# All splits on VectorE, the residual's product in PSUM, and a square with a scalar operand

## The chip, the cores and the metric

One core of a Trainium2 chip runs the whole program. The metric is device time in microseconds of one execution; three runs of the kernel before took 1109.92, 1103.96 and 1104.01 us, median 1104.01.

## What is computed

256 tokens of width 1024 go through two layers of a first block and one layer of a second, all in fp32. A layer of the first block is a mixer (a gated delta rule over four heads beside a dilated attention over eight) and a feed-forward part with a depthwise convolution, each between two norms:

```python
for l in range(2):
    h = rmsnorm(x, pre_mix_norm[l])
    h = hybrid_mixer(h, ...)                   # products with w_in, chunks, attention, w_out
    x = x + rmsnorm(h, post_mix_norm[l])
    h = rmsnorm(x, pre_ffn_norm[l])
    h = conv_glu_ffn(h, ffn_up[l], ffn_conv[l], ffn_conv_bias[l], ffn_down[l])
    x = x + rmsnorm(h, post_ffn_norm[l])
hn = rms_norm(x, mix_norm_g)                   # the second block
x = x + concat(gla(hn), conv(hn), diff_attention(hn)) @ w_out_2
x = x + hier_moe(rms_norm(x, ffn_norm_g))      # best of 4 groups, then 2 of its 4 experts
```

## The kernel before

The stages follow one another: mixer1, ffn, mixer1, ffn, mixer2, moe. Every product is made with both operands cut into a rounded head and the rest, its tail: `mm3` issues three matmuls, head by head (L404), head by tail (L405) and tail by head (L406). A weight tile of 128 x 1024 comes by one DMA on the queue of SyncE into a raw tile `wr` (in the MoE also into `yh`, `yl`, `grow` or `hres`); ScalarE copies the head `wh` (L382), and then VectorE or GpSimd subtracts it from the raw tile and so makes the tail `wl` (L383). This subtraction is the split. Heads and tails have five buffers each.

Who makes a split is set by numbers at the top. `POOLED0 = 2` and `POOLED = 5` give GpSimd the first splits of `tok_first`, with which a mixer or feed-forward stage begins; `POOL1 = 10` and `POOL2 = 2` give it every tenth of the other splits of mixer1 and every second of mixer2; in the MoE it has all four of expert 0's first matrix, one of four (`KPOOL = (1,)`) of the 15 other experts', and the rows themselves (`XPOOL = 2`).

Between two stages stands a boundary, for each of the two token tiles (the first rows, the second rows): ScalarE sums the squares of the stage's output, which lies in two PSUM banks (L415), VectorE multiplies that output by a gain and writes the product to `hres` in SBUF (L487), takes a reciprocal root in a chain of one-column instructions (`rsqrt1`, L342 to L350, with the square y * y at L344), and adds the scaled product to the residual `x` (L491). TensorE transposes the new rows (L326), ScalarE and VectorE make their heads and tails (`xh` L358, `xl` L359), and `tok_first` multiplies: first five weight tiles with the first rows (30 matmuls), then the same with the second rows. The last products of the stage before, for the second rows, are held back to run while the first rows go through the boundary. There are four such boundaries; the MoE begins with a residual step of its own (`route`, L1568).

The program's text lists several chains and one stream of filling products in one order (`Weave`); the framework then lays out each engine's queue from that order and from estimated durations. An engine runs its queue strictly in order.

Of the kernel before, what the change touches and what calls it, by code (L numbers as in the profile page):

```python
# [10 lines left out]
F32 = mybir.dt.float32  # L11
# [26 lines left out]
AFTER = 4  # L38
KPOOL = (1,)
GAT = 1  # L40
XPOOL = 2
CUT0 = ((0, 512),)
CUT1 = ((512, 768), (768, 1024))
YUP = True
RSQ = (1.0, -0.5, 0.37499722695340487, -0.3125009091063101, 0.27502146815610246, -0.24676164253236588)
HOLD = None
LAG = True
# [6 lines left out]
LAGE = 2  # L54
POOLED0 = 2
FIRST = 1
# [7 lines left out]
OUT2 = (4, 5, 6, 7, 2, 3, 0, 1)  # L64
POOLED = 5
POOL1 = 10
POOL2 = 2
POOLF = 0
# [129 lines left out]
class Weave:  # L198
    """Lays several dependent chains and one stream of filling work into one trace order."""

# [47 lines left out]
def emit(ctx, tc, A, out, stop=None, dbg=None):  # L248
# [89 lines left out]
    def rsqrt1(ss, scale, o=None):  # L338
        """1 / sqrt(sum * scale + EPS) of one value a partition, whose sum comes in two parts."""
        c = tmp([P, 5], tag="rs1")  # L340
        u, y, q, e, v = (c[:, i:i + 1] for i in range(5))
        V.tensor_scalar(u, ss[:, 0:1], ss[:, 1:2], EPS / scale, op0=OP.add, op1=OP.add)  # L342
        V.tensor_scalar(y.bitcast(I32), u.bitcast(I32), -0.5, 1597463007.0, op0=OP.mult, op1=OP.add)
        V.tensor_tensor(q, y, y, op=OP.mult)  # L344
        V.tensor_scalar(e, q, u, 1.0, op0=OP.mult, op1=OP.subtract)
        V.tensor_scalar(v, e, RSQ[5], RSQ[4], op0=OP.mult, op1=OP.add)
        for i in (3, 2, 1, 0):
            V.tensor_scalar(v, v, e, RSQ[i], op0=OP.mult, op1=OP.add)
        r = v if o is None else o
        V.tensor_scalar(r, v, y, scale ** -0.5, op0=OP.mult, op1=OP.mult)  # L350
        return r

    def split(h, l, src, gain=None, eng=V):
        if gain is None:
            SC.copy(h, src)
            eng.tensor_tensor(l, src, h.bitcast(F32), op=OP.subtract)
        else:
            i = SC.activation(h, src, AF.Identity, scale=gain)  # L358
            j = V.scalar_tensor_tensor(l, src, gain, h.bitcast(F32), op0=OP.mult, op1=OP.subtract)  # L359
            return i.ins, j.ins  # L360
# [10 lines left out]
    def weight(ap, eng=None, first=False, raw=None, to=None):  # L371
        if eng is None:
            share[1] += 1
            eng = G if share[0] and share[1] % share[0] == 0 else V
        if raw is None:
            raw = raw_tile()
            nc.sync.dma_start(raw, ap)
        h, l = to or (wp.tile([P, 1024], F32R, name=nm("wh"), tag="wh", bufs=WH),
                      wp.tile([P, 1024], F32R, name=nm("wl"), tag="wl", bufs=WH))
        last = gate.pop() if gate else None  # L380
        with tc.issue_after(last) if last else ExitStack():
            heads[:] = [(V.tensor_copy if first else SC.copy)(h, raw).ins]  # L382
        eng.tensor_tensor(l, raw, h.bitcast(F32), op=OP.subtract)  # L383
        return h, l
# [8 lines left out]
    def narrow_gen(p, w, xT):  # L393
        """The products of a few columns; rows n and on of the output hold the low part's share."""
        xh, xl = xT
        n = w.shape[2]
        for k in range(KT):
            T.matmul(p[:n, :S], w[:, k, :], xh[:, k, :], start=k == 0, stop=False)
            T.matmul(p[:n // 2, :S], w[:, k, :n // 2], xl[:, k, :], start=False, stop=k == KT - 1)
            if k % 4 == 3:  # L400
                yield 0.9
# [16 lines left out]
    def rows_in(t, xT, a, g, gain, done):  # L418
        """The residual step of token tile t, and its new rows, transposed and split."""
        xh, xl = xT  # L420
# [22 lines left out]
    def row_scales(nv, done, lag):  # L443
        """What the next norm scales the rows by: per row, and the same spread over the partitions."""
        rv, hv, R = nv
# [34 lines left out]
    def residual(t, a, g):  # L480
        """x += rmsnorm(a) * g on token tile t."""
        ss = square_sum(lambda n: a[t][n], 2)
        h2 = tmp([P, 2, 512], tag="hres", bufs=1)
        hs = [h2[:, n] for n in range(2)]
        for n in range(2):
            with tc.issue_after(marks[0][HOLD[n]][1]) if t and HOLD and HOLD[n] is not None else ExitStack():
                V.tensor_tensor(hs[n], a[t][n], g[n], op=OP.mult)  # L487
        r = rsqrt1(ss, 1.0 / D)
        for n in range(2):
            ns = slice(n * 512, (n + 1) * 512)  # L490
            V.scalar_tensor_tensor(x[:, t, ns], hs[n], r, x[:, t, ns], op0=OP.mult, op1=OP.add)  # L491

# [20 lines left out]
    def tok_first(ps, chunks, xT, done, end, mid=None, ahead=None):  # L513
        """Two groups of products of token rows; those of the first rows go ahead of the second rows' norm."""
        xh, xl = xT
# [617 lines left out]
    def mixer2(before, held, a0):  # L1133
# [149 lines left out]
        def gla():  # L1283
# [23 lines left out]
            def level_x(X, half, t):  # L1307
                """The keys' and queries' factors of four levels on token tile t; the last level reaches over the tiles."""
                c0 = half * (4 + t)
# [189 lines left out]
    def onehot(o, v, idx):  # L1499
        """The first greatest of four, as a one-hot row; and its value."""  # L1500
        n = v.shape[1]
# [10 lines left out]
    def moe(held, a):  # L1512
# [26 lines left out]
        def gather(gp, ps, t):  # L1539
            """Token tile t's share of the rows of groups 2 gp and 2 gp + 1."""  # L1540
            for n, src in enumerate((xsh, xsl)):
# [20 lines left out]
        def route():  # L1562
            for t in range(NT):
# [41 lines left out]
                if t == 1:  # L1605
                    gather(0, got, 1)
                    yield (1.8, 0.1)

        early = [weight(A["egu"][0, kk], G if kk % 2 else V,
                        to=[tmp([P, D], F32R, tag=tag, bufs=2) for tag in ("yh", "yl")]) for kk in range(EARLY)]  # L1610
        whl = tmp([P, NT, 2, 5], F32R, tag="whl", bufs=1)

        def shares(t):
            """What each expert of its group gives to a row; the softmax's sum over four cancels in the two greatest's shares."""
            yield lambda: ("goh", t) in done
# [42 lines left out]
        def slot_values(p, g):  # L1658
            """What the tokens give to the slots of a group: an expert's share times the row's scale, and the scale."""
            for t in range(NT):  # L1660
                T.matmul(p, sel[:, t, g, :], whl[:, t].rearrange("p j e -> p (j e)"), start=t == 0, stop=t == NT - 1)
# [30 lines left out]
        def up(e, between):  # L1692
# [3 lines left out]
            for kk in range(4):  # L1696
                if e == 0 and kk < EARLY:
                    w = early[kk]
                else:
                    with later(2 if e == 1 and kk < AFTER else 0):  # L1700
                        w = weight(A["egu"][e, kk], G if e == 0 or kk in KPOOL else V, raw=raws.pop(("up", e, kk), None))
                wh, wl = (v.rearrange("p (k c) -> p k c", k=2) for v in w)
# [57 lines left out]
        def rest():  # L1760
            """The tokens of a group past its 128 slots; no more than one group has any."""
            g0 = nc.values_load(firsti[0:1, 1:2], min_val=0, max_val=12,
# [169 lines left out]
```

## Time and profile before

| | us |
|---|---|
| median of three runs | 1104.01 |
| span of the profiled execution | 1100.8 |
| TensorE busy | 1052.8 |
| VectorE busy | 904.2 |
| ScalarE busy | 634.5 |
| GpSimd busy | 209.9 |
| mean granted TensorE clock | 0.960 |

The profile is of one execution; its span runs from the first instruction to the last, so it is a little shorter than the time of a run. Busy time is a sum over stages with different limits; a stage is read from its own window.

### The profile page before, as it was taken

To read this page: it belongs to the slowest core of one execution; us is meant where nothing else is said; L and a number is where in the kernel's file an instruction comes from. 1 tells how busy PE (TensorE), PEld (TensorE's weight loads), DVE (VectorE), ACT (ScalarE), POOL (GpSimd) and SP (SyncE) were. 2 spreads that over 40 slices of the span, in tenths; PEclk is the share of its full clock that TensorE was granted. 3 is DMA by queue.
4 is the path that set the end of the run, shared out by engine and by line. 5 is a ranking of instruction groups with operands and counts; after the bars stand their busy time and mean duration, and the time that the engine had idled before them with its cause. 6 is when DMAs were issued, how large, how long until landed. Compare 5 with 4: busy or idle time off the path is not lost.

```text
span 1100.8 us, 17299 instructions
## 1 busy us (share of the span) xinstructions
PE 1052.8 (96%) x6156; PEld 900.5 (82%) x6156; DVE 904.2 (82%) x2073; ACT 634.5 (58%) x1139; POOL 209.9 (19%) x175
## 2 busy tenths in 40 slices
PE   8999999999999899999899999998899997999997
PEld 7879877899999788887679999996777776887785
DVE  6797797798888879868797988888889768888886
ACT  6554455666655665535466665556554234787773
POOL 3510004100000462000140000004423415123231
PEclk9999998999999999999989999999889679999999
DMA  8642025555555453401437556555532036398892
GB/s 318 216 134 77 2 94 177 190 190 174 189 179 188 153 191 117 133 21 39 153 118 225 174 180 187 189 188 157 163 106 77 20 114 233 102 333 320 320 348 89
DMA packets 51997, 181.07 MB, mean 164 GB/s; under 512 B 6050, under 2 KB 7491, under 8 KB 51907
## 3 DMA queue, kind: packets, MB, share of 16 engines
q1 hardware_dynamic: 51186, 179.33, 48.7%
q8 instruction: 50, 0.82, 0.3%
q10 hardware_dynamic: 720, 0.59, 0.2%
q14 instruction: 41, 0.33, 0.1%
HBM read 178.86 MB, written 1.05 MB: 163 GB/s over the span
## 4 chain that ended last, share of the span: by engine, by line
PE 82%; DVE 12%; ACT 2%; issue 2%; DMA 1%; POOL 0%; SPq 0%; DVEq 0%; ACTq 0%
PE b L405 22%; PE b L404 22%; PE b L406 21%; PE b L326 4%; DVE wl L383 2%; PE b L1353 2%; PE b L884 2%; DVE x L491 2%; PE b L859 2%; PE b L918 1%; DVE cy L727 1%; PE b L576 1%; PE b L1544 1%; ACT wh L382 1%; PE b L575 1%
## 5 line engine op out<-in xcount | busy, mean ns | idle before, releaser
L382 ACT CAST wh<-wr 128x1024 fp32r<-128x1024 f32 x277 | 290.2, 1049 | 202.0 <-PE b L405 95.5
L383 DVE TENSOR_TENSOR wl<-wr,wh 128x1024 fp32r<-128x1024 f32 x225 | 287.2, 1280 | 65.5 <-ACT wh L382 62.7
L383 POOL TENSOR_TENSOR wl<-wr,wh 128x1024 fp32r<-128x1024 f32 x53 | 132.9, 2515 | 747.9 <-ACT wh L382 611.8
L404 PE MATMUL b<-xh,wh 128*128 128x256 f32 x816 | 237.9, 292 | 0.2 <-ACT tokq L1470 0.2
L406 PE MATMUL b<-xh,wl 128*128 128x256 f32 x816 | 234.3, 287 | 0.0
L405 PE MATMUL b<-xl,wh 128*128 128x256 f32 x816 | 233.8, 286 | 0.0
L404 PEld LDWEIGHTS b<-xh,wh 128*128 128x128 f32 x816 | 159.0, 195 | 4.0 <-issue 2.4
L405 PEld LDWEIGHTS b<-xl,wh 128*128 128x128 f32 x816 | 159.1, 195 | 1.7 <-issue 0.5
L406 PEld LDWEIGHTS b<-xh,wl 128*128 128x128 f32 x816 | 158.8, 195 | 0.4 <-issue 0.2
L404 PE MATMUL b<-wh,xh 128*128 128x512 f32 x256 | 107.7, 424 | 3.3 <-DVE wh L382 2.3
L404 PE MATMUL b<-wh,mh 128*128 128x512 f32 x272 | 110.4, 406 | 0.0
L405 PE MATMUL b<-wl,mh 128*128 128x512 f32 x272 | 109.4, 402 | 0.0
L406 PE MATMUL b<-wh,ml 128*128 128x512 f32 x272 | 108.5, 399 | 0.0
L405 PE MATMUL b<-wl,xh 128*128 128x512 f32 x256 | 106.8, 418 | 0.3 <-DVE wl L383 0.2
L406 PE MATMUL b<-wh,xl 128*128 128x512 f32 x256 | 105.2, 412 | 0.0
L1081 DVE SCALAR_TENSOR_TENSOR fu<-fq,par,fu 128x255 f32<-128x255 f32 (+1 forms) x144 | 69.1, 480 | 2.1
L404 PEld LDWEIGHTS b<-wh,xh 128*128 128x128 f32 x256 | 50.6, 198 | 16.6 <-issue 3.7
L406 PEld LDWEIGHTS b<-wh,ml 128*128 128x128 f32 x272 | 52.2, 192 | 11.4 <-issue 0.3
L404 PEld LDWEIGHTS b<-wh,mh 128*128 128x128 f32 x272 | 52.5, 193 | 10.7 <-ACT half L609 0.3
L405 PEld LDWEIGHTS b<-wl,xh 128*128 128x128 f32 x256 | 50.6, 198 | 12.8 <-issue 3.0
L405 PEld LDWEIGHTS b<-wl,mh 128*128 128x128 f32 x272 | 52.4, 193 | 10.2 <-issue 0.9
L406 PEld LDWEIGHTS b<-wh,xl 128*128 128x128 f32 x256 | 50.6, 198 | 11.4 <-issue 0.6
(431 smaller groups left out, 1970.2 us busy)
## 6 DMA issues: line engine op xcount, KB each, us to landing
wr<-in_win SPq DMA_DIRECT2D x78, 512.0 KB, 3.6
wr<-in_up SPq DMA_DIRECT2D x72, 512.0 KB, 3.5
wr<-in_down SPq DMA_DIRECT2D x44, 512.0 KB, 3.5
wr<-in_egu SPq DMA_DIRECT2D x44, 512.0 KB, 6.0
wr<-in_wout SPq DMA_DIRECT2D x24, 512.0 KB, 3.5
wr<-in_uptok SPq DMA_DIRECT2D x16, 512.0 KB, 4.3
mh<-in_edn SPq DMA_DIRECT2D x8, 1024.0 KB, 5.0
ml<-in_edn SPq DMA_DIRECT2D x8, 1024.0 KB, 5.1
```

The source lines that it names most:

```text
L326: T.transpose(o, i, ident[:i.shape[0], :i.shape[0]])
L382: heads[:] = [(V.tensor_copy if first else SC.copy)(h, raw).ins]
L383: eng.tensor_tensor(l, raw, h.bitcast(F32), op=OP.subtract)
L404: T.matmul(o, ah, bh, start=start, stop=False)
L405: T.matmul(o, ah, bl, start=False, stop=False)
L406: T.matmul(o, al, bh, start=False, stop=stop)
L491: V.scalar_tensor_tensor(x[:, t, ns], hs[n], r, x[:, t, ns], op0=OP.mult, op1=OP.add)
L575: T.matmul(p[:, 0:128], qT[:, 0:128], kT[:, 0:128], start=True, stop=True)
L859: T.matmul(pq[:, u * 64:(u + 1) * 64], atu[:, u, 0, :], tv[:, u, :, 0, :], start=True, stop=True)
L884: T.matmul(pq[:, 256 + u * 64:256 + (u + 1) * 64], RRu[:, u, :], pn[:, u, :], start=True, stop=True)
L1081: V.scalar_tensor_tensor(u[:, d:], p[:, :S - d], cw[:, 2 - d:3 - d], u[:, d:], op0=OP.mult, op1=OP.add)
L1353: T.matmul(p[:, j * S + t * 128:j * S + t * 128 + 128], Xl[hp, ts], Xl[hp, ts], start=True, stop=True, tile_position=(32 * h, 0))
```

## The change

All splits go to VectorE: `KPOOL`, `XPOOL`, `POOLED0`, `POOLED`, `POOL1` and `POOL2` become empty or zero, and expert 0's rule for GpSimd goes. The new helper `low` could cut a GpSimd split into four pieces; no call of it has GpSimd as its engine any more. In `residual` the product with the gain is written back to the PSUM bank that it is read from, so `hres` is not used there (it stays a raw tile of the MoE), and L491 reads its first operand from PSUM. In `rsqrt1` the square y * y is a `tensor_scalar` with y as its per-partition scalar, where it was a `tensor_tensor`. GpSimd keeps the spread of the row scales (L453, L455), the ropes (L980 to L985), a mask (L799) and factors of the gated linear attention (L1321 to L1324).

By place the splits that move are: 4 in the first mixer1, 5 at the boundary to each feed-forward part and to the second mixer1, 3 more inside that mixer1, 5 at the boundary to mixer2 and 12 inside it, 4 of expert 0, 2 of the rows and 15 of the other experts: 60.

```diff
-KPOOL = (1,)
+KPOOL = ()
-XPOOL = 2
+XPOOL = 0
-HOLD = None
+PIECES = 4
-POOLED0 = 2
+POOLED0 = 0
-POOLED = 5
-POOL1 = 10
-POOL2 = 2
+POOLED = 0
+POOL1 = 0
+POOL2 = 0
...
-        V.tensor_tensor(q, y, y, op=OP.mult)
+        V.tensor_scalar(q, y, y, None, op0=OP.mult)
...
+    def low(l, src, h, eng):
+        n = PIECES if eng is G else 1
+        w = src.shape[-1] // n
+        for i in range(n):
+            c = slice(i * w, (i + 1) * w)
+            eng.tensor_tensor(l[..., c], src[..., c], h[..., c].bitcast(F32), op=OP.subtract)
...
     def split(h, l, src, gain=None, eng=V):
         if gain is None:
             SC.copy(h, src)
-            eng.tensor_tensor(l, src, h.bitcast(F32), op=OP.subtract)
+            low(l, src, h, eng)
...
-        eng.tensor_tensor(l, raw, h.bitcast(F32), op=OP.subtract)
+        low(l, raw, h, eng)
...
         ss = square_sum(lambda n: a[t][n], 2)
-        h2 = tmp([P, 2, 512], tag="hres", bufs=1)
-        hs = [h2[:, n] for n in range(2)]
         for n in range(2):
-            with tc.issue_after(marks[0][HOLD[n]][1]) if t and HOLD and HOLD[n] is not None else ExitStack():
-                V.tensor_tensor(hs[n], a[t][n], g[n], op=OP.mult)
+            V.tensor_tensor(a[t][n], a[t][n], g[n], op=OP.mult)
         r = rsqrt1(ss, 1.0 / D)
         for n in range(2):
             ns = slice(n * 512, (n + 1) * 512)
-            V.scalar_tensor_tensor(x[:, t, ns], hs[n], r, x[:, t, ns], op0=OP.mult, op1=OP.add)
+            V.scalar_tensor_tensor(x[:, t, ns], a[t][n], r, x[:, t, ns], op0=OP.mult, op1=OP.add)
...
-                        w = weight(A["egu"][e, kk], G if e == 0 or kk in KPOOL else V, raw=raws.pop(("up", e, kk), None))
+                        w = weight(A["egu"][e, kk], G if kk in KPOOL else V, raw=raws.pop(("up", e, kk), None))
```

## Rows read from the trace of the kernel before

**Rows 1.** The page: its head and part 1, busy us (share of the span) xinstructions.
```profile
span 1100.8 us, 17299 instructions
...
PE 1052.8 (96%) x6156; PEld 900.5 (82%) x6156; DVE 904.2 (82%) x2073; ACT 634.5 (58%) x1139; POOL 209.9 (19%) x175
```

**Rows 2.** The page, part 5: line engine op out<-in xcount | busy us, mean ns | idle before, releaser.
```profile
L383 DVE TENSOR_TENSOR wl<-wr,wh 128x1024 fp32r<-128x1024 f32 x225 | 287.2, 1280 | 65.5 <-ACT wh L382 62.7
L383 POOL TENSOR_TENSOR wl<-wr,wh 128x1024 fp32r<-128x1024 f32 x53 | 132.9, 2515 | 747.9 <-ACT wh L382 611.8
```

**Rows 3.** Groups by form on VectorE (columns as before); last, the timeline: start us, us, instruction.
```profile
L383 DVE TENSOR_TENSOR wl<-ml,wh 128x1024 fp32r<-128x1024 f32 x16 | 18.8, 1211 | 0.0
...
L359 DVE SCALAR_TENSOR_TENSOR ml<-b,par,mh 128x512 fp32r<-128x512 f32 x6 | 4.5, 749 | 5.2 <-ACT mh L358 5.2
...
L345 DVE TENSOR_SCALAR rs<-rs 128x1 f32<-128x1 f32 x20 | 4.2, 211 | 0.5
...
961.33 2.35 DVE L383 TENSOR_TENSOR wl<-ml,wh 128x1024 fp32r<-128x1024 f32 x2
```

**Rows 4.** Two lines alone: instructions xcount: ns min/median/max, first and last start us.
```profile
L491 DVE SCALAR_TENSOR_TENSOR x<-hres,rs,x x16: 737/1958/2828, 179.1 to 764.5; 128x512 f32<-128x512 f32 x16
...
L344 DVE TENSOR_TENSOR rs<-rs x20: 149/159/2399, 20.7 to 927.8; 128x1 f32<-128x1 f32 x20
```

**Rows 5.** The chain that ended last: the page's shares, then pieces (start us, us).
```profile
PE b L405 22%; PE b L404 22%; PE b L406 21%; PE b L326 4%; DVE wl L383 2%; PE b L1353 2%; PE b L884 2%; DVE x L491 2%; PE b L859 2%; PE b L918 1%; DVE cy L727 1%; PE b L576 1%; PE b L1544 1%; ACT wh L382 1%; PE b L575 1%
...
152.73 2.29 DVE sm L1006
...
179.06 4.51 DVE x L491 x2
...
751.57 5.03 DVE x L491 x2
...
927.85 2.23 DVE rs L344
```

**Rows 6.** Waits of TensorE: who waited for whom, us in total, times, longest.
```profile
PE b L326 <- DVE x L491: 11.4, 8, 2.6
```

**Rows 7.** Timeline of the first feed-forward boundary: start us, us, instruction [idle before].
```profile
175.41 1.43 DVE L487 TENSOR_TENSOR hres<-b,grow 128x512 f32<-128x512 f32 x2 [3.13 <-ACT half L415]
...
177.86 5.15 POOL L383 TENSOR_TENSOR wl<-wr,wh 128x1024 fp32r<-128x1024 f32 x2 [4.88 <-ACT wh L382]
...
183.61 1.11 PE L326 MATMUL b<-cst,x 128*128 128x128 f32 x4 [2.03 <-DVE x L491]
...
184.97 0.80 PE L404 MATMUL b<-wh,xh 128*128 128x512 f32 x1 [0.24 <-ACT xh L358]
...
186.18 4.74 POOL L383 TENSOR_TENSOR wl<-wr,wh 128x1024 fp32r<-128x1024 f32 x2 [3.18 <-ACT wh L382]
...
189.30 2.83 DVE L491 SCALAR_TENSOR_TENSOR x<-hres,rs,x 128x512 f32<-128x512 f32 x2
```

**Rows 8.** Timeline of VectorE at mixer2's entry: the first and last of four.
```profile
772.69 1.23 DVE L622 TENSOR_SCALAR hs<-hs 128x8 f32<-128x8 f32 x1
...
786.56 1.63 DVE L622 TENSOR_SCALAR hs<-hs 128x8 f32<-128x8 f32 x1
```

**Rows 9.** Windows: us, busy us (xinstructions) of each engine, TensorE's clock, DMA share, GB/s.
```profile
184.90:192.65 7.75, 7.68 (x23) 6.10 (x24) 7.27 (x24) 6.13 (x17) 4.74 (x2) 0.67 0.65 188
174.00:192.00 18.00, 15.54 (x58) 11.97 (x57) 15.69 (x36) 10.70 (x25) 9.88 (x4) 0.81 0.47 146
766.00:790.00 24.00, 20.99 (x110) 17.48 (x109) 23.39 (x67) 15.37 (x27) 12.95 (x8) 1.00 0.60 195
960.00:1018.00 58.00, 57.97 (x261) 46.69 (x260) 51.22 (x50) 47.67 (x59) 16.08 (x7) 1.00 0.90 322
```

**Rows 10.** Waits of VectorE in 960 to 1018 us: us in total, times, longest.
```profile
DVE wl L383 <- ACT wh L382: 3.1, 9, 0.5
DVE hd L1715 <- ACT sg L1713: 2.8, 4, 0.8
```

More of the change, by code (lines that the diff above doesn't have):

```diff
@@ L1607, in route @@
                     yield (1.8, 0.1)
-        early = [weight(A["egu"][0, kk], G if kk % 2 else V,
+        early = [weight(A["egu"][0, kk], V,
                         to=[tmp([P, D], F32R, tag=tag, bufs=2) for tag in ("yh", "yl")]) for kk in range(EARLY)]
```

## The prediction

> **What bounds the kernel now.** The page's first part: TensorE is busy 96% of the span, VectorE 82%, GpSimd 19% [rows 1]. TensorE is the bound nearly everywhere, so VectorE's work counts only where TensorE stands still for it. The windows show where: in the middle of the MoE TensorE is busy 57.97 of 58.00 us at full clock with VectorE at 51.22; at the first feed-forward boundary it is busy 15.54 of 18.00 at a mean clock of 0.81, 3.4 us of clock lost [rows 9].
>
> TensorE's waits name who it stands still for: above all the new residual `x` of L491, 11.4 us in 8 waits [rows 6]. L491 is a short instruction made long: the quickest of its 16 took 0.737 us, the median 1.958, the longest 2.828; of the one-element square L344 the median is 0.159 us and the longest 2.399 [rows 4]. The timeline of the first boundary shows why: GpSimd starts two splits at 177.86 (5.15 us together) [rows 7], two L491 start inside them at 179.06 and take 4.51 [rows 5], and the transposes that need them start at 183.61 after TensorE idled 2.03 us; the first product follows at 184.97 [rows 7]. So a GpSimd split holds up a VectorE instruction that reads two operands from SBUF, for as long as the split lasts. The chain that ended last is full of this: ten single VectorE instructions of 2.2 to 2.7 us, from the L1006 at 152.73 to the L344 at 927.85, and L491 pairs of 4.5, 4.5 and 5.0 us [rows 5].
>
> [...]
>
> **The change, part by part.**
>
> *Splits off GpSimd.* 60 leave it: 53 that read `wr`, 5 of other raw tiles and 2 of the MoE's rows (`XPOOL`). One takes 2.515 us there [rows 2]. On VectorE an undisturbed one takes 1.211 us, and two back to back 2.35, so 1.14 of the engine's time each [rows 3]: 68.4 us more work. The stalls that go are of that size, so VectorE's 904 us hardly move; what counts is how much of either lies on the chain.
>
> (1) Nine of the ten single stalls lie away from the boundaries, 21.4 us long in all. Their own work is between 9 x 0.16 (L344's median) and 9 x 0.72 us (half the L487 pair's 1.43 [rows 7], as wide as any of them): I take 3, so 18.4 us of stall go. But the split behind each was in flight just then: its head `wh` is ready, and VectorE finds it in its queue at that very place. It costs 0 if it falls into an idle moment and 1.14 if it stands before a link of the chain. The page counts 2% of the span, 22 us or 19 of VectorE's own 270 splits, on the chain [rows 5], which speaks for few; the place, a chain just stalled, for most. I take six of nine: 18.4 - 6.8 = 11.6 us gained, bounds 8.1 and 18.4.
>
> (2) The entry of mixer2, 766 to 790 us: VectorE is busy 23.39 of 24.00 [rows 9], with four stalled instructions from 772.69 to 786.56 [rows 8], 7.6 us in all, whose own work is about 0.17 each (as L344's): 6.9 us of stall against four moved splits at 1.14 = 4.6. Gain 2.3 us.
>
> (3) The four residual boundaries. In the first, VectorE works without a break from 175.41 (L487) to 192.13 (the end of the second rows' L491), 16.7 us [rows 7]. The stalls in it are 4.51 - 1.4 and 2.83 - 1.4, 4.5 us. Four splits move into this very stretch (two from 177.86, two from 186.18 [rows 7]; `tok_first`'s fifth comes before it): 4 x 1.14 = 4.6. So the second rows' `x` comes when it came before. What improves is the first rows' `x`: it ends at 180.5 if no split stands before it, at 182.8 if two do, in place of 183.57. Its 30 products (6.7 us, at the MoE's 261 matmuls in 58 us [rows 9]) are then through before the second rows are there, where in the trace only 23 of them had begun when the second rows' transposes came [rows 9]: the other seven, 1.6 us, are the most a boundary can give. [...] So 0 to 1.6 us each; I take 1: 4 us for four.
>
> (4) The start of the MoE: four splits of expert 0 and the two of the rows, 6 x 1.14 = 6.8 us, come into the routing chain, which was held up for about 3 us beside the L344 already counted. Between -3 and +6.8; I take +2.
>
> (5) The middle of the MoE: 15 splits, seven in the window 960 to 1018. VectorE's 51.22 + 7 x 1.14 = 59.2 us in 58 if no stall went away; but its splits are held up there too (mean 1.280 over the kernel against 1.211 [rows 2, 3]), and its idle time is in-order waiting on ScalarE, 3.1 and 2.8 us [rows 10], which a busier queue uses up. I take 0, covered by the five buffers of heads and tails; without that cover 1.2 us in 58.
>
> *The product in PSUM.* L487 writes to the bank that it reads; no VectorE instruction of the trace writes PSUM. Bounds: 0.72 as now and 0.749 as the nearest 512-wide row with a PSUM operand [rows 3]; I take no change. L491 then reads one operand from PSUM: 0.749 against 0.737, 16 x 0.012 = 0.2 us. The banks stay taken until L491; the next that need them are the second rows' products, behind L491 anyway. L487 starts only behind ScalarE's squares of the same bank already, so writing there adds no wait. [...]
>
> *The square with a scalar operand.* 20 times 0.211 (as L345, one column with a per-partition scalar [rows 3]) in place of 0.159 [rows 4]: 1.0 us. That GpSimd can't hold it up is worth little once the splits are gone.
>
> Sum: -11.6 - 2.3 - 4 + 2 + 0.2 + 1.0 = -14.7 us. The profiled span is 1100.8 us [rows 1], 3.2 under the median of 1104.0 of the runs shown, so 1086.1 in a profile and 1089.3 in a run.
>
> **The rivals.** The stalls on the chain come to 18.4 + 6.9 + 18 (four boundaries of 4.5) + 3 = 46 us, and every moved split on the chain gives back 1.14. With N of them the change is 1.14 N - 46 + 1.2; my sum has N = 26. The queue of VectorE is laid out anew, so N is what I know least.
> [...]
> B. *The gaps close and the clock holds.* The splits fall into VectorE's 197 idle us [rows 1]: -18.4 - 2.3 - 6.4 + 1.2 = -26, and with the boundaries' clock near 1 (3.4 us in the first [rows 9]) some 6 more: 1072 us. Against it: at the boundaries VectorE has no idle time.
> C. *VectorE becomes the bound: slower.* From N = 40 the gain is gone, from N = 50 it is over 1% slower. That needs the MoE's 15 splits on the chain, where the in-order waits would have to stay in full (59.2 + 5.9 = 65 us in 58). With N = 55 it is +18, 1122 us. Against it: TensorE hardly waits there now.
>
> **How the numbers follow.** Forecast 0.46 (its own range 1081 to 1097), A 0.28, B 0.15, C 0.11. A measurement of this kernel can tell about 1% (11 us) from no change. Faster by over 1% is under 1093: B and some five sixths of the forecast, 0.53. Slower is C, 0.11; the rest, 0.36, is A and the forecast's upper end. The range leaves out the far ends of B and C: 1070 to 1108.
>
> **What would show it.** Right: L491 all near 0.75 us and the square near 0.21; VectorE busy about 905 us; TensorE's waits on `x` below 6 us, part of them now before the second rows; VectorE splits in the chain where single stalls stood; the MoE's middle unchanged. Wrong: TensorE under 57 of 58 us in the MoE's middle or waits on `wl` there (C), no clock lost at the boundaries (B), or L491 still near 2 us, which would mean that something other than GpSimd's splits held it.

## The result, and the profile after

The changed kernel takes 1072.85 us (median of four runs, 1068.41 to 1077.21), beside 1105.68 for the kernel before in the same series: 0.9705 of it, with an interval of 0.9658 to 0.9752. Run once more with others, the same kernel had 0.9721 (0.9681 to 0.9761). The forecast was 1089.3, so direction and range held, and the gain of 33 us is more than twice the 14.7 forecast. Runs over 1.5% longer than the fastest of their kernel are left out of all ratios here; the medians of the table of experiments count them (two of the six with three boundaries, and two of the seven of the kernel before in one series).

The page of the profiled execution, the quickest of the four (columns as in [rows 1, 2]):

```profile
span 1066.6 us, 17279 instructions
...
PE 1031.6 (97%) x6156; PEld 882.3 (83%) x6156; DVE 893.8 (84%) x2133; ACT 636.3 (60%) x1139; POOL 56.2 (5%) x115
...
L359 DVE TENSOR_TENSOR wl<-wr,wh 128x1024 fp32r<-128x1024 f32 x278 | 340.0, 1227 | 64.7 <-ACT wh L390 60.8
```

Line numbers have moved: the split is L359, the head L390, the three matmuls of `mm3` L412 to L414, the residual's product L492 and its last step L496. The square is still L344. Against [rows 1] the span is 34.2 us shorter. The same 6156 matmuls kept TensorE busy 21.2 us less (1052.8 to 1031.6), and its idle time, span less busy, fell by 13.0 (48.0 to 35.0). VectorE, with 60 splits more, is busy 10.4 us less (904.2 to 893.8): its instructions are no longer made long.

Two lines alone (ns min/median/max), and TensorE's wait for the new `x`:

```profile
L496 DVE SCALAR_TENSOR_TENSOR x<-b,rs,x x16: 739/743/752, 176.5 to 745.1; 128x512 f32<-128x512 f32 x16
...
L344 DVE TENSOR_SCALAR rs<-rs x20: 196/211/216, 19.0 to 898.2; 128x1 f32<-128x1 f32 x20
```

```profile
PE b L326 <- DVE x L496: 7.4, 4, 2.4
```

These answer [rows 4] and [rows 6]: the residual step's median fell from 1.958 to 0.743 us, the longest square from 2.399 to 0.216, and eight waits of 11.4 us became four of 7.4, one at each boundary.

Where the time went shows when both traces are cut into the same ten stretches of TensorE's work. The limits are chosen so that each pair of rows holds the same matmuls (x803 and x803, x622 and x622, and so on). First before, then after; columns as in [rows 9].

```profile
0.00:130.00 130.00, 122.74 (x803) 106.36 (x804) 99.32 (x265) 70.70 (x162) 27.29 (x42) 0.99 0.46 158
130.00:240.00 110.00, 106.59 (x622) 90.26 (x621) 91.22 (x267) 65.62 (x120) 18.25 (x10) 0.97 0.45 149
240.00:400.00 160.00, 157.02 (x993) 141.66 (x992) 136.07 (x249) 97.17 (x163) 20.07 (x16) 0.99 0.56 176
400.00:500.00 100.00, 97.44 (x689) 86.81 (x688) 77.49 (x212) 50.13 (x119) 16.22 (x24) 0.98 0.32 105
500.00:640.00 140.00, 134.18 (x787) 114.78 (x787) 116.58 (x309) 82.88 (x148) 18.32 (x10) 0.96 0.47 150
640.00:775.00 135.00, 130.42 (x827) 117.70 (x826) 114.59 (x216) 81.90 (x142) 17.03 (x12) 0.99 0.56 177
775.00:800.00 25.00, 21.09 (x117) 18.82 (x116) 20.64 (x58) 12.17 (x18) 9.27 (x5) 0.86 0.51 167
800.00:895.00 95.00, 91.15 (x424) 70.55 (x423) 75.97 (x204) 36.74 (x76) 26.92 (x37) 0.78 0.21 67
895.00:975.00 80.00, 74.31 (x397) 60.39 (x396) 68.38 (x193) 50.19 (x93) 25.62 (x11) 0.96 0.54 188
975.00:1100.80 125.80, 117.85 (x516) 93.21 (x514) 103.91 (x110) 87.03 (x106) 30.93 (x12) 0.99 0.75 279
```

```profile
0.00:126.19 126.19, 121.11 (x803) 105.66 (x804) 98.67 (x268) 71.38 (x162) 19.86 (x39) 1.00 0.49 167
126.19:233.11 106.92, 104.28 (x622) 87.99 (x621) 91.04 (x273) 65.61 (x120) 1.63 (x4) 1.00 0.49 153
233.11:391.91 158.80, 156.28 (x993) 140.39 (x992) 134.45 (x254) 97.35 (x163) 6.81 (x11) 1.00 0.56 177
391.91:489.28 97.37, 96.40 (x689) 85.15 (x688) 77.51 (x214) 50.00 (x119) 12.15 (x22) 1.00 0.35 107
489.28:622.83 133.55, 131.35 (x787) 112.64 (x787) 114.16 (x315) 82.94 (x148) 1.62 (x4) 0.99 0.50 157
622.83:755.69 132.86, 130.25 (x827) 117.76 (x826) 112.59 (x221) 81.88 (x141) 2.89 (x6) 0.99 0.56 178
755.69:773.91 18.22, 18.13 (x117) 15.95 (x116) 16.83 (x62) 12.75 (x19) 0.14 (x1) 1.00 0.55 192
773.91:861.20 87.29, 84.05 (x424) 63.91 (x422) 71.63 (x210) 36.85 (x76) 11.07 (x30) 0.88 0.21 67
861.20:943.10 81.90, 72.96 (x397) 59.16 (x396) 68.83 (x205) 50.70 (x92) 0.00 (x0) 0.98 0.55 198
943.10:1066.60 123.50, 116.79 (x516) 93.65 (x514) 108.04 (x122) 86.82 (x106) 0.00 (x0) 0.98 0.75 283
```

Subtracting pair by pair (idle is length less TensorE's busy time; clock is TensorE's mean granted clock, first number of the last three in a row above):

| stretch (before) | what lies in it | length | idle | busy | clock |
|---|---|---|---|---|---|
| 0 to 130 | start, first attention | -3.8 | -2.2 | -1.6 | 0.99 to 1.00 |
| 130 to 240 | stall of L1006, boundary 1 | -3.1 | -0.8 | -2.3 | 0.97 to 1.00 |
| 240 to 400 | boundary 2 | -1.2 | -0.5 | -0.7 | 0.99 to 1.00 |
| 400 to 500 | stall of L762 | -2.6 | -1.6 | -1.0 | 0.98 to 1.00 |
| 500 to 640 | stalls of L336 and L955, boundary 3 | -6.5 | -3.6 | -2.8 | 0.96 to 0.99 |
| 640 to 775 | boundary 4 | -2.1 | -2.0 | -0.2 | 0.99 to 0.99 |
| 775 to 800 | mixer2's entry | -6.8 | -3.8 | -3.0 | 0.86 to 1.00 |
| 800 to 895 | gated linear attention (GLA), two stalls | -7.7 | -0.6 | -7.1 | 0.78 to 0.88 |
| 895 to 975 | three stalls, start of the MoE | +1.9 | +3.3 | -1.4 | 0.96 to 0.98 |
| 975 to end | rest of the MoE | -2.3 | -1.2 | -1.1 | 0.99 to 0.98 |
| all | | -34.2 | -13.0 | -21.2 | 0.960 to 0.983 |

Three fifths of the gain are TensorE doing the same matmuls in less time, most of it in stretches where the granted clock was lower before. The mean clocks agree: by them 4.0% of 1100.8 us were lost before and 1.7% of 1066.6 after, an estimate of 44 and 18 us, 26 apart. One stretch got longer: the start of the MoE, into which splits moved.

### The profile page after: what moved, and what is told of

Read it like the earlier page. It is cut to its first block, busy times and chain, and to the rows that moved or that the text cites. A ratio compares the mean times of both kernels' runs of the same rounds, so it can differ in the third digit from the quotient of the medians.

```text
span 1066.6 us, 17279 instructions
## 1 busy us (share of the span) xinstructions
PE 1031.6 (97%) x6156; PEld 882.3 (83%) x6156; DVE 893.8 (84%) x2133; ACT 636.3 (60%) x1139; POOL 56.2 (5%) x115
## 4 chain that ended last, share of the span: by engine, by line
PE 86%; DVE 8%; issue 3%; ACT 2%; DMA 0%; POOL 0%; DVEq 0%; POOLq 0%; ACTq 0%
PE b L412 23%; PE b L413 23%; PE b L414 23%; PE b L326 4%; DVE wl L359 2%; PE b L889 2%; PE b L864 2%; PE b L581 1%; PE b L923 1%; PE b L580 1%; DVE cy L732 1%; PE b L1358 1%; ACT wh L390 1%; PE b L603 1%; PE b L1760 1%
## 5 line engine op out<-in xcount | busy, mean ns | idle before, releaser
L390 ACT CAST wh<-wr 128x1024 fp32r<-128x1024 f32 x277 | 290.0, 1049 | 195.0 <-PE b L413 93.6
L359 DVE TENSOR_TENSOR wl<-wr,wh 128x1024 fp32r<-128x1024 f32 x278 | 340.0, 1227 | 64.7 <-ACT wh L390 60.8
L412 PE MATMUL b<-xh,wh 128*128 128x256 f32 x816 | 236.6, 290 | 0.2 <-ACT tokq L1475 0.2
L414 PE MATMUL b<-xh,wl 128*128 128x256 f32 x816 | 233.1, 286 | 0.0
L412 PEld LDWEIGHTS b<-xh,wh 128*128 128x128 f32 x816 | 157.9, 194 | 3.3 <-issue 1.5
L414 PEld LDWEIGHTS b<-xh,wl 128*128 128x128 f32 x816 | 157.9, 194 | 0.5 <-issue 0.3
L412 PE MATMUL b<-wh,mh 128*128 128x512 f32 x272 | 108.9, 401 | 2.5 <-ACT mh L363 2.5
L412 PE MATMUL b<-wh,xh 128*128 128x512 f32 x256 | 107.1, 420 | 3.7 <-ACT xh L366 1.3
L414 PE MATMUL b<-wh,ml 128*128 128x512 f32 x272 | 107.0, 394 | 0.0
L413 PE MATMUL b<-wl,xh 128*128 128x512 f32 x256 | 103.2, 408 | 1.3 <-DVE wl L359 1.3
L414 PE MATMUL b<-wh,xl 128*128 128x512 f32 x256 | 103.6, 408 | 0.0
L412 PEld LDWEIGHTS b<-wh,xh 128*128 128x128 f32 x256 | 49.2, 192 | 19.1 <-ACT xh L366 5.6
L412 PEld LDWEIGHTS b<-wh,mh 128*128 128x128 f32 x272 | 51.6, 190 | 13.0 <-ACT mh L363 2.7
L414 PEld LDWEIGHTS b<-wh,ml 128*128 128x128 f32 x272 | 51.5, 189 | 11.6 <-issue 0.3
L414 PEld LDWEIGHTS b<-wh,xl 128*128 128x128 f32 x256 | 49.3, 193 | 11.7 <-issue 1.1
L412 PE MATMUL b<-wh,xgh 128*128 128x512 f32 x128 | 51.8, 405 | 0.0
```

Of the source, the lines that this page charges most:

```text
L359: eng.tensor_tensor(l[..., c], src[..., c], h[..., c].bitcast(F32), op=OP.subtract)
L412: T.matmul(o, ah, bh, start=start, stop=False)
L413: T.matmul(o, ah, bl, start=False, stop=False)
L414: T.matmul(o, al, bh, start=False, stop=stop)
```

## The experiments

Theory L says that a GpSimd instruction holds up a VectorE instruction that reads two operands from SBUF, and that ending this is the whole gain. Its rivals: D, that GpSimd's tails simply came late; E, that the two small edits carry the gain; C, that VectorE is crowded in the MoE. All medians in one table; ratios are to the kernel before in the same series, the last four columns from the profiled execution of each. Kernels are compared by the ratios.

| kernel | median us | ratio (interval) | span | TensorE busy | idle | clock |
|---|---|---|---|---|---|---|
| before | 1105.68 | 1 | 1100.8 | 1052.8 | 48.0 | 0.960 |
| after | 1072.85 | 0.9705 (0.9658 to 0.9752) | 1066.6 | 1031.6 | 35.0 | 0.983 |
| after, again | 1072.65 | 0.9721 (0.9681 to 0.9761) | 1067.2 | 1033.0 | 34.2 | 0.980 |
| splits alone | 1068.73 | 0.9705 (0.9623 to 0.9788) | 1065.2 | 1032.3 | 32.9 | 0.982 |
| both edits alone | 1084.30 | 0.9861 (0.9781 to 0.9941) | 1077.7 | 1035.7 | 42.0 | 0.974 |
| product alone | 1092.80 | 0.9900 (0.9845 to 0.9954) | 1091.8 | 1051.7 | 40.1 | 0.959 |
| splits twice | 1123.05 | 1.0193 (1.0092 to 1.0293) | 1118.7 | 1057.8 | 60.9 | 0.960 |
| GpSimd as a shadow | 1137.29 | 1.0349 (1.0258 to 1.0439) | 1132.5 | 1050.6 | 81.9 | 0.967 |
| GpSimd in pieces | 1081.16 | 0.9804 (0.9748 to 0.9860) | 1077.0 | 1041.0 | 36.0 | 0.969 |
| MoE back | 1075.65 | 0.9727 (0.9669 to 0.9785) | 1074.0 | 1038.4 | 35.6 | 0.974 |
| mixers back | 1090.03 | 0.9872 (0.9821 to 0.9923) | 1089.3 | 1046.7 | 42.6 | 0.966 |
| three boundaries on GpSimd | 1058.11 | 0.9572 (0.9518 to 0.9627) | 1054.5 | 1025.5 | 29.0 | 0.986 |
| four boundaries on GpSimd | 1051.29 | 0.9551 (0.9503 to 0.9600) | 1050.2 | 1022.3 | 27.9 | 0.990 |

### GpSimd as a shadow: is it the held engine or the late tail?

```diff
 def low(l, src, h, eng):
-    n = PIECES if eng is G else 1
-    ... eng.tensor_tensor(l[..., c], src[..., c], ...)
+    V.tensor_tensor(l, src, h.bitcast(F32), op=OP.subtract)
+    if eng is G:                   # the moved splits, but not the rows'
+        G.tensor_tensor(src, src, h.bitcast(F32), op=OP.subtract)
```

> The changed kernel, with 58 of the moved splits (all but the two of the rows) made by VectorE and then once more by GpSimd, in place in the raw tile, which nobody reads afterwards. The tails come as early as in the changed kernel; only GpSimd's work is back beside VectorE. Theory L (GpSimd's work as such holds VectorE up): the stalls come back, 40 to 46 us of them, with VectorE instructions of 2 to 2.8 us, and the time with them: 1095 to 1115 us. Rival D (the tails came late from GpSimd, 2.5 us against 1.2, and TensorE waited for them): 1072 to 1078 us, as in the changed kernel.

1137 us. From the page, the groups on GpSimd, and the chain that ended last:

```profile
PE 1050.6 (93%) x6156; PEld 891.6 (79%) x6156; DVE 970.6 (86%) x2133; ACT 636.7 (56%) x1139; POOL 205.1 (18%) x173
```

```profile
L357 POOL TENSOR_TENSOR wr<-wr,wh 128x1024 f32<-128x1024 f32 x53 | 135.7, 2562 | 788.9 <-DVE wl L355 338.8 <-DMA wr<-in_win 164.6 <-DVE rsq_b L335 83.9
```

```profile
422.72 2.30 DVE u L765
...
816.68 2.49 DVE yc L1250
```

Nobody reads what GpSimd makes here (only the raw tile comes free later), and still VectorE is busy 76.8 us more with the same instructions, single ones of 2.3 to 2.5 us are back on the chain, and TensorE's idle time rises by 46.9 us. Rival D falls: what a GpSimd split costs is the held VectorE, not the late tail. (In the trace of the kernel before, TensorE waited for a tail of GpSimd's once, for 0.5 us.) The time went past the range of L too: here the 60 splits stay on VectorE and are held themselves. By the groups of the trace some 41 of the 76.8 us are VectorE's own splits (those of `wr` take 1.355 us in the mean, 1.227 in the changed kernel), which GpSimd made by itself in the kernel before. The later raw tiles add little: ScalarE's waits for a weight to land sum to 6.9 us, beside 3.3 in the changed kernel. The two instructions of the chain above, 2.30 and 2.49 us, are about as long as a GpSimd split, 2.562 us.

### Splits alone, both edits alone, product alone

```diff
 # splits alone: the changed kernel with
+    h2 = tmp([P, 2, 512], tag="hres", bufs=1)       # product to SBUF again
+    V.tensor_tensor(q, y, y, op=OP.mult)            # square as it was
 # both edits alone: the changed kernel with
+KPOOL = (1,); XPOOL = 2; POOLED0 = 2; POOLED = 5; POOL1 = 10; POOL2 = 2; PIECES = 1
+    w = weight(..., G if e == 0 or kk in KPOOL else V, ...)
 # product alone: as both edits alone, and
+    V.tensor_tensor(q, y, y, op=OP.mult)
```

> The changed kernel with its two small edits undone: the residual's product goes to SBUF and the square is a tensor_tensor again; all splits stay on VectorE. Theory L (the held VectorE): GpSimd's splits held VectorE's two-operand instructions up, and taking them away is the whole gain. It expects 1070 to 1075 us (about 1072), within 2 us of the changed kernel, with L491's successor near 0.74 us and the square near 0.16. Rival E (the edits): the PSUM product and the scalar operand carry the boundaries' part of the gain, 7 to 12 us; it expects 1080 to 1085 us, and instructions of the boundary near 2 us where GpSimd still works.

> The kernel before with the two small edits alone: the splits stay on GpSimd, whole. Theory L, in the form that only instructions with two SBUF operands are held: the residual's last step and the squares are no longer held, near 0.75 and 0.21 us, so the boundaries give about 1.8 us each and the squares some 4, about 1094 us (1090 to 1098); the other stalls (single instructions near mixer2, the GLA and the attention) stay. If any VectorE instruction with an SBUF operand is held, nothing changes: 1103 to 1108 us with the residual step still near 2 us. Rival E expects the boundaries' stalls gone and half the gain or more: 1085 to 1090.

> The kernel before with the product in PSUM alone: the splits stay on GpSimd and the square stays a tensor_tensor. Theory S expects nearly all that the two edits gave together (0.986 of before): the four boundaries' residual steps near 0.75 us, the long square (2.2 to 2.4 us) still there at the second boundary and at the routing, so 1 to 4 us more than the two edits together: 0.986 to 0.990 of before. If the scalar operand carries the gain: 0.995 to 1.0.

With the splits gone from GpSimd the edits bring nothing that shows: 0.9705 with and without them. So rival E falls as the cause of this gain, though its own number for the edits alone was the better one: on the kernel before they bring 1.4% (1084.30 us, where E had 1085 to 1090 and L 1090 to 1098). The product without the square brings 1.0%, as expected of it. So the edits are a second cure for part of the same stalls. With both edits alone, the first boundary reads (timelines of GpSimd, VectorE and TensorE; start us, us):

```profile
178.08 4.74 POOL L359 TENSOR_TENSOR wl<-wr,wh 128x1024 fp32r<-128x1024 f32 x2 [4.87 <-ACT wh L390]
...
179.34 1.41 DVE L496 SCALAR_TENSOR_TENSOR x<-b,rs,x 128x512 f32<-128x512 f32 x2
...
180.83 1.03 PE L326 MATMUL b<-cst,x 128*128 128x128 f32 x8
```

In [rows 5, 7] the same pair, inside the same two GpSimd splits, took 4.51 us and TensorE idled 2.03. With one operand in PSUM it takes 1.41 inside 4.74 us of GpSimd work, and TensorE does not wait. For the other edit, the same square at the second boundary, first with the product alone, then with both edits; under each the GpSimd splits beside it:

```profile
368.88 2.40 DVE L344 TENSOR_TENSOR rs<-rs 128x1 f32<-128x1 f32 x1
...
368.87 4.71 POOL L359 TENSOR_TENSOR wl<-wr,wh 128x1024 fp32r<-128x1024 f32 x2 [2.94 <-ACT wh L390]
```

```profile
368.93 0.22 DVE L344 TENSOR_SCALAR rs<-rs 128x1 f32<-128x1 f32 x1
...
368.92 4.74 POOL L359 TENSOR_TENSOR wl<-wr,wh 128x1024 fp32r<-128x1024 f32 x2 [3.02 <-ACT wh L390]
```

Both start within 0.01 us of a split's start; the `tensor_tensor` is held to the split's end (2.40 us), the `tensor_scalar` of one column is not (0.22). Behind this place the same matmuls start 3.3 us later with the product alone. The profiled spans differ by 14.1 us in the end, the rest of it mostly at the GLA and the routing, and all of it in TensorE's busy time (1051.7 against 1035.7; idle time is 1.9 less): clock, which no run here separates from the square. The profile with both edits is the quickest of its four runs, and the two ratios, 0.9861 and 0.9900, lie inside each other's intervals, so that the square is worth anything in the whole time is not shown.

### The moved splits made twice

```diff
+    for _ in range(2 if eng is G else 1):           # constants as before, all on VectorE
+        V.tensor_tensor(l, src, h.bitcast(F32), op=OP.subtract)
```

> The changed kernel, but VectorE makes each of the 60 moved splits twice (the same subtraction into the same tile), so 68 us more work on VectorE at 1.14 us each. It counts how many of the 60 lie on the path that sets the end. The recorded sum had 26: that expects 26 x 1.14 = 30 us more than the changed kernel, about 1103 us. The rival that the splits fall into VectorE's idle time (none to five on the path) expects 0 to 6 us more, 1073 to 1079 us.

```profile
PE 1057.8 (95%) x6156; PEld 898.4 (80%) x6156; DVE 952.6 (85%) x2193; ACT 634.6 (57%) x1139; POOL 64.5 (6%) x115
```

```profile
PE b L326 <- DVE x L493: 14.4, 4, 4.9
```

Fifty us more than the changed kernel: both expectations missed. TensorE's idle time rose by 25.9 us, near the 30 of the recorded sum, but its busy time rose by 26.2 as well, with the clock back at 0.960. The sum priced a split on the chain at its own length; with the busy time that went with it, the second 60 cost about twice that. The wait for `x` doubled, from 7.4 to 14.4 us, so at the boundaries the splits do lie on the path: 1.75 us for each of four. VectorE has no room for a second 60. How many of the first 60 lie on the path this run does not count by itself.

### GpSimd back in parts, and in pieces

```diff
 # MoE back                          # mixers back        # pieces: both edits alone, but
+KPOOL = (1,); XPOOL = 2             +POOL1 = 10          +PIECES = 4
+... G if e == 0 or kk in KPOOL ...  +POOL2 = 2
```

> The changed kernel with the MoE's splits (expert 0's four, one of four of the 15 other experts', the two of the rows) back on GpSimd, whole. The recorded sum (routing 2 us dearer with the splits on VectorE, the middle unchanged) expects 2 us less than the changed kernel, 1069 to 1072 us. The traces of before and after put the routing at +1.9 and the middle and end at -2.4 us: no change, 1071 to 1075. Rival C (VectorE crowded in the MoE by the 21 splits) expects 1060 to 1067 us; if the held instructions of GpSimd's splits cost more there than the splits on VectorE: 1077 or more.

> The changed kernel with the splits inside the mixers back on GpSimd, whole: every tenth of the other splits of mixer1, every second of mixer2's. These lie away from the residual steps, beside one-column and 128x8 chains, the attention's and the GLA's instructions that read two operands from SBUF. Theory L expects the single stalls of 2.2 to 2.7 us back, and with them what the stretches between the boundaries gained from before to after (about 1.2 at the first attention, 2.6 and 4 to 5 in the second mixer1, some 8 of mixer2's 14): 1084 to 1092 us. The recorded sum, in which six of nine stalls were replaced by a split of half the length, expects 9 to 12 us more than the changed kernel's 1072: 1081 to 1084. Rival D (no stall, only later tails): 1070 to 1076.

> The kernel before with the two small edits and each of GpSimd's splits cut into four pieces of 128x256. If a VectorE instruction waits only for the GpSimd instruction in flight, a stall is at most a piece long, near 0.65 us in place of 2.2: two thirds of the single stalls go, 1066 to 1076 us. If VectorE waits until GpSimd has no more such work queued, the stalls stay near 2.2 us: 1082 to 1088 us, as the two edits alone (0.986 of before).

MoE back changes nothing that can be measured (0.9727 beside 0.9721 for the changed kernel in the same series): C falls, and so does the idea that the routing's 2 us could be had back this way. Mixers back loses more than half of the whole gain (0.9872) with 21 splits, two more than the kernel before had there: the count of every second split of mixer2 now takes in the boundary's own, and two of the 21 lie at that boundary. L's range, taken from the stretches of the table, held it; the recorded sum's 1081 to 1084 was too low. In pieces, VectorE's timeline at mixer2's entry, GpSimd's beside it, and the group on GpSimd:

```profile
755.66 0.77 DVE L627 TENSOR_SCALAR hs<-hs 128x8 f32<-128x8 f32 x1
756.46 0.67 DVE L332 TENSOR_SCALAR hr<-hs 128x8 int32<-128x8 int32 x1
757.16 0.66 DVE L334 TENSOR_TENSOR rsq_a<-hr 128x8 f32<-128x8 f32 x1
757.85 0.66 DVE L335 SCALAR_TENSOR_TENSOR rsq_b<-rsq_a,hs 128x8 f32<-128x8 f32 x1
```

```profile
755.67 4.92 POOL L359 TENSOR_TENSOR wl<-wr,wh 128x256 fp32r<-128x256 f32 x7
```

```profile
L359 POOL TENSOR_TENSOR wl<-wr,wh 128x256 fp32r<-128x256 f32 x212 | 175.5, 863 | 703.8 <-ACT wh L390 578.5 <-DVE sm L1015 83.2 <-DVE gsc L1375 22.3
```

The median fell between the two expectations. A stall is now one piece long, as L says, but a run of narrow instructions is held once at each: four in a row near 0.7 us, whose own length in the changed kernel is 0.15 to 0.17. And a split in four pieces takes GpSimd 4 x 0.863 = 3.45 us in place of 2.5. Pieces on GpSimd (0.9804) are not told from whole splits there (0.9861, intervals overlapping), and lose to splits on VectorE (0.9705).

### Both cures, each where it works

Splits at the boundaries lie on VectorE's path (the doubled run: 14.4 us of waits for `x` where the changed kernel has 7.4); GpSimd's splits there no longer hold the residual step (both edits alone: none of the 16 L496 over 0.752 us). So the changed kernel, with the boundary splits alone back on GpSimd:

```diff
+PIECES = 1
+POOLED = 5
-def tok_first(..., mid=None, ahead=None):
+def tok_first(..., mid=None, ahead=None, pooled=POOLED):
-    ... G if len(ws) < (POOLED0 if mid else POOLED) else None ...
+    ... G if len(ws) < (POOLED0 if mid else pooled) else None ...
 # in mixer2
+    yield from tok_first(ps, (w[10:14], w[14:18]), xT, done, end, pooled=0)   # three boundaries
+    yield from tok_first(ps, (w[10:14], w[14:18]), xT, done, end, pooled=4)   # four boundaries
```

> The changed kernel once more, beside the others of this call: 1068 to 1077 us by its first runs, 0.9705 of the kernel before.

> The changed kernel with the five splits at each of three boundaries (to both feed-forward parts and to the second mixer1) back on GpSimd, whole. Theory S (two cures for one stall): with its product in PSUM the residual step reads one operand from SBUF and isn't held, so there the splits cost VectorE nothing on GpSimd and up to 1.14 us each on VectorE. The traces so far show these three boundaries 3.1, 2.9 and 2.1 us or more shorter with the splits on GpSimd and the product in PSUM than in the changed kernel: 8 to 10 us less, 1061 to 1065 us, and no wait of TensorE on the new x over 1 us there. The rival, that any GpSimd split beside a boundary holds VectorE up again (the one-column chain, the tails of the rows), expects 1075 to 1085 us.

> The kernel of f1_three_boundaries with four of the five splits at the fourth boundary (to mixer2) on GpSimd as well. Theory S: they run while the residual step works, which isn't held, and are through before mixer2's narrow 128x8 chains begin some 10 us later, so the wait of 2.4 us for the new x goes, and the stretch of half clock behind it: 3 to 4 us less than 0.957 of before, 0.953 to 0.955, about 1053 to 1056 us. The rival, that they run on into the narrow chains and hold those up as in the kernel before: 1058 to 1064 us.

Three boundaries give 0.9572 of before, where the changed kernel has 0.9721 in the same series: a larger gain than theory S's 1061 to 1065 us (the median is 1058.11). With the fourth it is 0.9551, at the upper edge of its expectation. The page of the last kernel, and the longest of TensorE's waits in the one with three:

```profile
PE 1022.3 (97%) x6156; PEld 876.3 (83%) x6156; DVE 878.8 (84%) x2114; ACT 634.8 (60%) x1139; POOL 106.7 (10%) x134
```

```profile
PE b L326 <- DVE hd L1720: 2.8, 1, 2.8
PE b L326 <- DVE x L496: 2.6, 2, 2.4
```

Of the four waits for `x`, 7.4 us, three are gone in the first of the two, all but 0.2 us of what is left being boundary 4's. The fourth boundary's gain (4.3 us of the profiled span) is inside the intervals of the two ratios, so that both are better than the changed kernel is shown, and that four are better than three is not.

## Why the prediction came out as it did

**The mechanism: right.** L496 at 0.743 us and the square at 0.211 are what the text asked for (0.75 and 0.21), and the shadow showed that it is GpSimd's work as such that holds VectorE (76.8 us more of busy time with the same instructions).

**The step that failed: the sum had no term for the clock.** Every term (1) to (5) was a time of waiting. The clock came in as the 3.4 us lost at the first boundary and as 6 us in rival B. Measured, the idle time fell by 13.0 us, close to the 14.7 forecast, and TensorE's busy time by 21.2 us besides. That the idle time comes so close is luck in part: the five stretches of terms (1) and (4) and of boundaries 1 and 3 lost 3.3 us of it where the text had 11.6, boundaries 2 and 4 lost 2.5 (2 in the text), mixer2's entry 3.8 (2.3), and 3.4 came from the start and the MoE's end, for which the sum had nothing. [Rows 9] showed the clock of the first boundary, 0.81; the window from 800 to 895 has 0.78 over 95 us, the largest single loss in the kernel, in a stretch that the prediction treated only as two stalls. That is where 7.1 us of the 21.2 lie.

**Term (1), nine stalls, -11.6, and term (4), the MoE's start, +2.** The stretches with the nine stalls and the MoE's start, the boundaries taken out, gave 1.3 + 2.6 + 5.2 + 7.7 - 1.9 = 14.9 us where the two terms had 9.6. (At 130 to 240 and 500 to 640 the boundary's share, 1.8 and 1.3, is read from where the same matmuls start in both timelines.) But of the 7.7 at the GLA only 0.6 is idle time: there the stall was not paid as a wait. At the routing, the one stretch that got longer, VectorE has 12 instructions more (x193 to x205) and TensorE 3.3 us more of idle time: that splits would cost there was right, and that three stalls go in the same stretch did not outweigh it.

**Term (2), mixer2's entry, -2.3: too small.** It gave 6.8, 3.8 of idle time and 3.0 of busy time at a clock of 0.86 before and 1.00 after.

**Term (3), the boundaries, -1 each: mechanism right, clock wrong.** VectorE's timeline of the changed kernel at the first boundary, then TensorE's:

```profile
172.91 1.22 DVE L359 TENSOR_TENSOR wl<-wr,wh 128x1024 fp32r<-128x1024 f32 x1
...
174.17 1.22 DVE L359 TENSOR_TENSOR wl<-wr,wh 128x1024 fp32r<-128x1024 f32 x1
...
175.92 0.69 DVE L492 TENSOR_TENSOR b<-b,grow 128x512 f32<-128x512 f32 x1
176.52 1.40 DVE L496 SCALAR_TENSOR_TENSOR x<-b,rs,x 128x512 f32<-128x512 f32 x2
...
177.40 1.22 PE L326 MATMUL b<-cst,x 128*128 128x128 f32 x8 [1.73 <-DVE x L496]
```

Two splits stand ahead of the first rows' `x`, as the second case of the text had it ("at 182.8 if two do"), so TensorE's wait only shrank from 2.03 to 1.73 us. No part of it came before the second rows, where the text looked for some: all four waits are for the first rows, and before the second rows TensorE does not wait for `x`. The 1 us taken out of "0 to 1.6 us each" allowed for a lower clock after a wait between the token tiles, the author's estimate, which no run shows. What the runs show of the clock after a wait for the first rows differs from place to place: after the 2.03 of the kernel before it was 0.67 over 7.75 us [rows 9]; after this 1.73 the clock stayed at 1.00 (0.97 over that stretch before); after a wait just as long at the third boundary, 1.73 us up to 541.75, it was 0.50 from 543.1 to 546.5. The four boundaries gave about 1.8, 1.2, 1.3 and 2.1 us, 6.4 in place of 4. Waits on `x` below 6 us, which the text asked for, did not come (7.4), but the product in PSUM has a part in that. The L492 above is a product of the second rows, and it stands ahead of the first rows' step, as one does at each boundary and two at the fourth. With splits alone, where the product goes to the one buffer of `hres`, it stands behind, and the waits are shorter at every boundary:

```profile
PE b L326 <- DVE x L498: 4.8, 4, 1.3
```

**Term (5) and the small edits.** The MoE's middle and end gave 2.3 us where 0 was taken; MoE back says that this cannot be measured. The product into PSUM made no instruction longer, though by the order just shown it cost some 2.6 us of waits (7.4 against 4.8), which the ratios do not show: L492 has a median of 0.694 us and L496 one of 0.743, against 0.750 with the product in SBUF (splits alone). The square went from 0.152 (splits alone) to 0.211 us, 20 times, 1.2 us where 1.0 was taken.

**What was not in the sum at all:** 3.8 us before the first boundary, where the start waits less and an L727 of 2.59 us at 71.07 is no longer held. VectorE's busy time came out at 893.8, 11 below the 905 of the text.

**Among the rivals** B, "the gaps close and the clock holds", at 1072 and a chance of 0.15, is what happened, with another division: less from the gaps (13 in place of 26) and more from the clock (21 in place of 6). That its time was met to 1 us is luck. The argument against it, that VectorE has no idle time at the boundaries, was sound for the waits there and said nothing of the clock elsewhere. The text also stopped short of its own finding: it held that a split holds up an instruction with two SBUF operands, and never asked what the PSUM product would be worth if the splits stayed where they were.

## What to carry to other kernels

Cut both traces at the same matmuls and split each difference into TensorE's idle and busy time before pricing anything: in this kernel 13.0 us of idle time went and 21.2 us of busy time with it, so a sum of waits alone was less than half of the gain. Where GpSimd and VectorE work side by side, look first for the VectorE instructions made long (here the residual step, a median of 1.958 us and 0.743 once it was free), and then choose between two cures: take the work off GpSimd (here it paid inside the mixers: 0.9872 of before with their splits on GpSimd, 0.9705 with them on VectorE), or give the held instruction an operand in PSUM and leave the work there (here it paid at the boundaries, where VectorE works without a break: 0.9572 against 0.9721). The two brought nothing on top of each other in one place (0.9705 with the splits alone and with both), and the best kernel here, 0.9551, used each in another.

## What the runs showed of the hardware

- *A one-column `tensor_scalar` was not held, one of eight columns was.* The 128x1 square of both edits took 0.22 us inside a GpSimd split, and none of its 20 took over 0.216, while in the run in pieces the two 128x8 `tensor_scalar` shown above took 0.77 and 0.67 us (0.164 in the changed kernel) beside a piece of 0.7.
- *Half clock in stretches that count as fully busy.* In the GLA of the kernel before, and in the first mixer of the run in pieces:

```profile
862.20:869.00 6.80, 6.80 (x38) 5.11 (x37) 5.06 (x10) 2.15 (x4) 3.79 (x8) 0.98 0.00 0
869.00:893.00 24.00, 24.00 (x79) 18.20 (x79) 14.59 (x31) 4.67 (x9) 3.20 (x2) 0.51 0.19 66
```

```profile
95.00:109.40 14.40, 14.40 (x125) 13.54 (x124) 9.36 (x19) 5.80 (x13) 0.00 (x0) 1.00 0.16 53
109.40:123.10 13.70, 13.70 (x61) 11.94 (x61) 6.60 (x29) 3.65 (x9) 0.00 (x0) 0.51 0.00 0
```

  As the profile counts it, TensorE was busy without a break before the clock fell to 0.51 and while it stayed there. In the second case the changed kernel does the same work at 1.00, and nothing in either trace says why this execution lost it; it cost an estimated 6.7 us (13.70 us at 0.51 in place of 1.00). So the clock's part of the gain is shown as a sum over executions, and that each microsecond of it was caused by a stall is not shown.
- *VectorE kept the order of its queue.* In the changed kernel it stood idle for 0.61 us, waiting for the `xgh` of one instruction, though the split behind it had had its head since 918.69 and no product that reads tails ran from 917.6 to 923.2:

```profile
920.30 0.88 DVE L367 SCALAR_TENSOR_TENSOR xgl<-b,par,xgh 128x256 fp32r<-128x256 f32 x2 [0.61 <-ACT xgh L366]
921.09 1.22 DVE L359 TENSOR_TENSOR wl<-hres,wh 128x1024 fp32r<-128x1024 f32 x1
```

- *The scatter between executions goes with the clock.* The four runs of the changed kernel, 1068.41, 1069.92, 1075.78 and 1077.21 us, had mean clocks of 0.983, 0.980, 0.975 and 0.971.
